# An event-driven list scheduler, DMA issues placed by their buffer, and weights copied back over three passes, in an eight-core encoder layer

## The chip, the cores and the metric

The kernel runs on all 8 NeuronCores of one Trainium2 chip, two of the 16 streams on each core, no exchange between cores. The metric is the device time of the slowest core in microseconds. Some executions here fell in a slower state, one die at a clearly lower granted TensorE clock (0.81 to 0.82 against 0.97 on the other die). In the lines of the profile PE is TensorE, PEld its loading of weights, DVE VectorE, ACT ScalarE and POOL GpSimd; SPq and POOLq are the queues of instructions in which SyncE (SP) and GpSimd issue DMA transfers. The granted clock is the clock that the profile records for TensorE, as a share of full speed.

## The reference, cut to what matters

```python
def layer(x, ...):                       # x: (B, T, 1024)
    z = rmsnorm(x, g_pre_mix) @ w_in     # 1024 -> 6 x 1024: xa, ga, u, v, two merge gates
    # branch A: width-4 causal conv -> RG-LRU scan over time -> * gelu(ga) -> @ w_br_a
    # branch B: gelu(u) * (Ws_masked @ LN(gelu(v)) + b_s), 128-position chunks -> @ w_br_b
    mix = (sigmoid(g_a) * o_a + sigmoid(g_b) * o_b) @ w_out
    x = x + rmsnorm(mix, g_post_mix)
    gate, up = split(rmsnorm(x, g_pre_ffn) @ w_ffn_in)          # 2 x 2816
    return x + rmsnorm((silu(gate) * up) @ w_ffn_out, g_post_ffn)
```

A core works on 4096 prompt rows and 64 sample rows, cut into nine tiles of 3 or 4 chunks of 128 rows. All weights, 70 pieces of at most 128 x 2048 elements, pass through a ring of 8 buffers once per tile. They lie in HBM in float32 (`wall`); a load from there casts to bf16 on the way (in the profile before 12.4 us, the median, from issue to landing). A bf16 copy (`wsc`) is written back to HBM in an early pass, and later tiles load that (4.6 us).

## The kernel before: the parts that the change touches

A recorder builds the program once without weights in time, to fix an order of stages, and replays that order. Each stage is a closure that appends instructions to in-order lists, one for each engine; semaphore waits follow from which buffers an instruction reads and writes.

```python
def load(i, pid):                                   # a piece into a ring buffer
    slot = free.popleft()
    if pid in cached:
        dma("sp", ...out=wring[slot], in_=wsc[pid]...)      # cached bf16 copy, by SP
        return
    dma("pool", ...out=wring[slot], in_=wall[pid]...)       # cast load, by GpSimd
    if seen[pid] == pid % 2:                                # copy back in pass 0 or 1
        cached.add(pid); todo_wo[i] = (slot, pid, n)

def fill():                                         # before every stage: as soon as a slot is released
    while not dry and free and W["next"] < len(stream):
        load(W["next"], stream[W["next"]]); W["next"] += 1

def acquire(pid):                                   # strictly in the order of the dry run
    assert stream[i] == pid
    if i in todo_wo: dma("sp", ...out=wsc[pid], in_=wring[slot]...)   # copy back at first use
...
def xr(s):       # x again, into the residual buffer x1 that the y store of the last tile reads
    dma("sp", ...out=x1[s], in_=x_rows(T, s)...)
put("xr", ("xr", t, s), xr, after=[("fb", t - 1, min(s, pns - 1))])
...
def gev(c):      # ScalarE: two gate tanh, then two exponentials, chunk by chunk
    tanh(E); tanh(I); exp(A, E); exp(E, E)
...
order = record(Prog(), None); P = Prog(); record(P, order)      # dry run, then replay
```

The constants of the spatial gate are loaded and multiplied out (16 pairs of small f32 matmuls, 64 records in the trace) before the first projection.

## Time and profile before

| | kernel before |
|---|---|
| median | 2448.1 us of 3 runs (2435.85 to 2545.6, the last a slow one) |
| TensorE busy, idle (core 0, 2440.1 us) | 2134 us, 306 us |
| mean granted clock, all cores | 0.951 to 0.957 |
| loads of weights | 105 cast, 525 cached, 70 copies back |

### The profile page before, as it was taken

What the parts mean: (1) busy time and instruction counts of PE and PEld (TensorE: products, weight loads), DVE (VectorE), ACT (ScalarE), POOL (GpSimd) and SP (SyncE); (2) the same over time, 40 slices, a digit from 0 to 9 for tenths busy, and PEclk for the clock granted to TensorE, in tenths of its full rate; (3) what the DMA queues carried; (4) which work ended last, traced back from release to release, by engine and by line L of the source; (5) the groups of instructions that cost most, each with busy time, mean ns of one, the idle gap of its engine ahead of it and who ended that gap; (6) DMA issues with size and microseconds to landing.
All of it is one profiled execution on the core that took longest, in us unless ns stands there. A gap on an engine that the chain in (4) does not pass through costs nothing.

```text
span 2440.1 us, 35711 instructions; the slowest of 8 cores (2422.7 to 2440.1 us)
## 1 busy us (share of the span) xinstructions
PE 2134.1 (87%) x10708; PEld 1037.8 (43%) x10708; DVE 1120.7 (46%) x1710; ACT 978.6 (40%) x1595; POOL 588.2 (24%) x966
## 2 busy tenths in 40 slices
PE   3788799679898899989998999899989988699795
PEld 2333344234343444434443444455545544354352
DVE  2653662116831386227832484258238427642231
ACT  2743651216612294126712481256229126611210
POOL 2213411234102240044104310331132033203302
PEclk9989899889998999999999999999999999899898
DMA  8588599885696544463545554556665664356351
GB/s 185 116 154 177 129 198 198 175 236 136 164 220 185 190 153 142 153 209 113 165 158 176 175 173 151 184 186 217 200 207 191 200 231 137 101 178 215 121 177 52
DMA packets 117308, 416.68 MB, mean 171 GB/s; under 512 B 14465, under 2 KB 14465, under 8 KB 117122
## 3 DMA queue, kind: packets, MB, share of 16 engines
q1 hardware_dynamic: 96592, 341.73, 43.2%
q0 software_dynamic: 19808, 71.05, 16.4%
q8 instruction: 92, 1.51, 0.3%
q10 hardware_dynamic: 722, 1.62, 0.2%
q14 instruction: 94, 0.77, 0.1%
HBM read 414.79 MB, written 53.54 MB: 192 GB/s over the span
## 4 chain that ended last, share of the span: by engine, by line
PE 67%; DMA 11%; DVE 6%; POOL 5%; ACT 5%; issue 5%; SPq 0%; DVEq 0%; POOLq 0%; ACTq 0%
PE ps L647 45%; PE ps L1126 11%; DMA wring<-wall 4%; PE ps L1031 4%; PE ps L868 4%; DMA wsc<-wring 2%; DMA wring<-wsc 2%; DVE xcf L750 1%; PE ps L602 1%; POOL x L1162 1%; DVE chI L803 1%; POOL stats L585 1%; DMA yp<-x 1%; DMA gvf<-rows 1%; POOL x L1157 1%
## 5 line engine op out<-in xcount | busy, mean ns | idle before, releaser
L647 PE MATMUL ps<-xnT,wring 128*128 128x512 bf16 (+2 forms) x2880 | 652.2, 377 | 109.5 <-DMA wring<-wsc 38.0
L647 PE MATMUL ps<-hnT,wring 128*128 128x512 bf16 (+2 forms) x3168 | 630.5, 361 | 13.4 <-DVE hnT L607 7.2
L647 PEld LDWEIGHTS ps<-xnT,wring 128*128 128x128 bf16 x2880 | 287.0, 101 | 418.5 <-issue 175.7
L647 PEld LDWEIGHTS ps<-hnT,wring 128*128 128x128 bf16 x3168 | 310.5, 98 | 323.7 <-issue 23.5
L1126 PE MATMUL ps<-wring,ffT 128*128 128x512 bf16 (+1 forms) x1452 | 318.7, 379 | 5.3 <-DMA wring<-wall 5.3
L1105 ACT ACTIVATE sgt<-ps 128x512 f32<-128x512 f32 (+2 forms) x198 | 109.0, 555 | 404.6 <-PE ps L647 392.8
L996 DVE SCALAR_TENSOR_TENSOR ffT<-ffT,ps 128x512 f32<-128x512 f32 (+2 forms) x144 | 88.8, 633 | 318.9 <-PE ps L647 246.0
L1109 DVE SCALAR_TENSOR_TENSOR sgt<-sgt,ps 128x512 f32<-128x512 f32 (+2 forms) x198 | 125.4, 633 | 222.8 <-PE ps L647 220.9
L987 ACT ACTIVATE ffT<-ps 128x512 f32<-128x512 f32 (+2 forms) x144 | 78.7, 553 | 357.6 <-PE ps L647 301.3
L1126 PEld LDWEIGHTS ps<-wring,ffT 128*128 128x128 bf16 (+1 forms) x1452 | 140.0, 98 | 182.1 <-issue 18.9
L750 DVE SCALAR_TENSOR_TENSOR xcf<-xa,vecs_sb,xcf 128x512 f32<-128x512 f32 (+2 forms) x240 | 161.0, 671 | 25.7 <-DVE xcf L750 0.5
L578 POOL TENSOR_SCALAR stats<-stats 128x1 f32<-128x1 f32 (+1 forms) x132 | 40.6, 308 | 526.5 <-ACT ffT L591 476.3
L1111 DVE SCALAR_TENSOR_TENSOR ffT<-sgt,ps 128x512 bf16<-128x512 f32 (+2 forms) x198 | 125.9, 636 | 41.1 <-PE ps L647 37.5
L1002 POOL TENSOR_TENSOR vnm<-ffT 128x512 bf16<-128x512 f32 (+2 forms) x72 | 83.8, 1164 | 248.3 <-DVE ffT L996 160.0
L647 PE MATMUL ps<-gsT,wring 128*128 128x512 bf16 (+2 forms) x576 | 131.7, 374 | 13.1 <-DVE gsT L950 5.2
L462 POOL DMA_DIRECT2D wring<-wall x105 | 58.9, 565 | 318.1 <-PE ps L647 274.1
L647 PE MATMUL ps<-hgT,wring 128*128 128x512 bf16 (+2 forms) x576 | 127.2, 365 | 4.1 <-DVE ffT L996 2.3
L1031 PE MATMUL ps<-wring,vnm 128*128 128x512 bf16 (+1 forms) x528 | 120.2, 384 | 3.2 <-POOL vnm L1002 2.5
L868 PE MATMUL ps<-wring,xnT 128*128 128x512 bf16 (+1 forms) x528 | 120.0, 382 | 1.4 <-ACT gga L823 1.4
L585 POOL TENSOR_TENSOR stats<-stats,nhalf 128x1 f32<-128x1 f32 x165 | 106.7, 647 | 25.4 <-POOL stats L578 1.0
L1153 DVE SCALAR_TENSOR_TENSOR tok<-ps,stats,gbc_pf 128x512 f32<-128x512 f32 (+1 forms) x33 | 24.6, 747 | 169.7 <-POOL stats L585 103.3
L1134 DVE COPY gvf<-ps 128x512 f32<-128x512 f32 (+1 forms) x33 | 22.0, 688 | 157.3 <-PE ps L1126 144.1
(113 smaller groups left out, 2230.0 us busy)
## 6 DMA issues: line engine op xcount, KB each, us to landing
wring<-wsc SPq DMA_DIRECT2D x511, 512.0 KB, 4.6
wring<-wall POOLq DMA_DIRECT2D x101, 512.0 KB, 12.4
wsc<-wring SPq DMA_DIRECT2D x68, 512.0 KB, 9.4
x<-xp SPq DMA_DIRECT2D x32, 512.0 KB, 4.6
yp<-x POOLq DMA_DIRECT2D x32, 512.0 KB, 3.7
xin<-xp SPq DMA_DIRECT2D x28, 512.0 KB, 5.8
wring<-wsc SPq DMA_DIRECT2D x14, 256.0 KB, 3.2
wring<-wall POOLq DMA_DIRECT2D x4, 256.0 KB, 14.2
```

The costliest lines, as they stand in the source:

```text
L585: pool(lambda e: e.tensor_tensor(out=stats[0:PT, r2:r2 + 1], in0=stats[0:PT, r:r + 1], in1=nhalf[0:PT, :], op=ALU.pow), 180, [("st", r), ( ...
L647: mm(lambda e, k=k: e.matmul(ps[:, b, 0:nt], lhsT=wv[:, k, m * 128:(m + 1) * 128], rhs=rhsT[:, k, 0:nt], start=(k == 0), stop=(k == NCH - ...
L750: dve(lambda e, k=k, dst=dst, win=win: e.scalar_tensor_tensor(out=dst, in0=win(k), scalar=vecs[:, V_CW + k, c:c + 1], in1=dst, op0=ALU.mul ...
L868: mm(lambda e, k=k, wv=wv, b=b: e.matmul(ps[0:PT, b, :], lhsT=xnT[:, k, col:col + PT], rhs=wv[:, k % 4, :], start=(k == 0), stop=(k == NCH ...
L987: act(lambda e: e.activation(out=tsig[i][:, 0:nt], in_=ps[:, b, 0:nt], func=AF.Tanh, scale=0.5), nt, [("ps", b)], c_tsig(i))
L996: dve(lambda e: e.scalar_tensor_tensor(out=mtmp[m][:, 0:nt], in0=tsig[i][:, 0:nt], scalar=1.0, in1=ps[:, b, 0:nt], op0=ALU.add, op1=ALU.mu ...
L1002: pool(lambda e: e.tensor_tensor(out=mixT[:, c, 0:nt], in0=mtmp[a][:, 0:nt], in1=mtmp[b][:, 0:nt], op=ALU.add), nt, c_mtmp(a) + c_mtmp(b), ...
L1031: mm(lambda e, k=k, n=n, wv=wv: e.matmul(ps[0:PT, pr + n, :], lhsT=mixT[:, k, col:col + PT], rhs=wv[:, k % 4, :], start=(k == 0), stop=(k ...
L1105: act(lambda e: e.activation(out=sgt[:, i, 0:nt], in_=ps[:, b, 0:nt], func=AF.Tanh, scale=0.5), nt, [("ps", b)], [("sgt", i)])
L1109: dve(lambda e: e.scalar_tensor_tensor(out=sgt[:, i, 0:nt], in0=sgt[:, i, 0:nt], scalar=1.0, in1=ps[:, bg, 0:nt], op0=ALU.add, op1=ALU.mul ...
L1111: dve(lambda e: e.scalar_tensor_tensor(out=ffT[:, j, 0:nt], in0=sgt[:, i, 0:nt], scalar=0.5, in1=ps[:, bu, 0:nt], op0=ALU.mult, op1=ALU.mu ...
L1126: mm(lambda e, j=j, kk=kk, b=b, PT=PT, col=col: e.matmul(ps[0:PT, b, :], lhsT=ffT[:, j, col:col + PT], rhs=wv[:, kk, :], start=(j == 0), s ...
```

## The change

Its intent: every engine takes, at each step, the stage that can start first (ties by a priority list); a DMA is put into its queue only when the model says its buffer is free; weight pieces may be used in any order in which they have landed; copies back are spread over three passes; x comes before the constants.

```diff
+def PASS_OF(pid):
+    return pid % 3
...
             def fill():
...
-                while not dry and free and W["next"] < len(stream):
+                at = P.free["pe"]
+                most = 0 if ("xsq", 0, 1) not in done else 2 if ("xsq", 0, 3) not in done else len(stream)
+                while wo and P.ready([("wr", wo[0])]) <= at:
+                    copy_back(wo.popleft())
+                while free and W["next"] < most and P.idle_from(("wr", free[0])) <= at:
...
             def acquire(pid):
-                assert stream[i] == pid
+                slot = have[pid].popleft()          # whichever piece has been loaded
+                if slot in todo_wo:
+                    wo.append(slot)                 # copy back later, when landed, at the latest when released
...
...
-                    put("xr", ("xr", t, s), lambda s=s: xr(s), after=[...])
+                    put("xr", ("xr", t, s), lambda s=s: xr(s), idle=lambda s=s: ("x1", s), after=[...])
...
+                def gex(c):                         # the two exponentials, now a stage of their own
...
-            order = record(Prog(), None)            # replay a fixed order
+            while True:                             # in the dry run and in the real one
+                fill()
+                for e in P.ENGS:
+                    on = [(r, PRI.index(n), q) ...  # stages open on this engine, earliest start r
+                    start = max(P.free[e], min(z[0] for z in on))
+                    best = ... min((z for z in on if z[0] <= start), key=priority + switch)
+                emit(best)
```

`switch` adds 8 places to the rank of a stage that would need another ScalarE table. For the first tile the scaling of x moves to VectorE, the carry copy of the scan moves from GpSimd to VectorE, and the spatial constants are built with 11 small f32 matmuls, after the first projections.

## The prediction

> **What bounds the kernel now.** I read the span of every core first (2422.7 to 2440.1 us, granted clock 0.951 to 0.957, both dies alike, so the profile is an undisturbed execution), then the busy shares, then stretches of the span, then the gaps of TensorE one by one, then what the DMA-issuing queue SP waits for.
>
> ```profile
> span 2440.1 us, 35711 instructions; the slowest of 8 cores (2422.7 to 2440.1 us)
> PE 2134.1 (87%) x10708; PEld 1037.8 (43%) x10708; DVE 1120.7 (46%) x1710; ACT 978.6 (40%) x1595; POOL 588.2 (24%) x966
> q1 hardware_dynamic: 96592, 341.73, 43.2%
> q0 software_dynamic: 19808, 71.05, 16.4%
> wring<-wall POOLq DMA_DIRECT2D x101, 512.0 KB, 12.4
> ```
>
> TensorE is idle for 2440 - 2134 = 306 us. A long run of 512-column matmuls goes at 215.8 ns each (288 in 62.16 us in the chain of waits) and of 384 columns at 162 ns (24 in 3.90 us). With the counts of the groups by shape: 6588 x 0.2158 = 1422; 2448 x 0.162 = 398; 816 of 448 columns x 0.189 = 154; 768 of 128 columns at about 0.056 = 43; 18 us of f32 setup. That is 2035 us, so of the 2134 busy us about 99 are matmuls at a slow clock. Idle plus slow clock, 405 us, is all that a reordering can win; the work itself does not shrink.
>
> The same counts split by stretches. I cut where the transposes of a tile's FFN input begin, since the work between two cuts is one tile's FFN and the next tile's branches.
>
> ```profile
> 0.00:61.00 61.00, 21.99 (x96) 17.70 (x96) 13.40 (x34) 15.36 (x22) 17.64 (x35) 1.00 0.86 185
> 61.00:76.00 15.00, 9.12 (x29) 3.47 (x29) 5.70 (x9) 5.97 (x10) 4.76 (x10) 0.90 0.66 202
> 76.00:122.00 46.00, 37.52 (x156) 15.75 (x154) 32.95 (x51) 39.41 (x57) 11.38 (x30) 0.91 0.50 88
> ...
> 367.00:460.00 93.00, 86.73 (x396) 37.79 (x395) 20.54 (x30) 12.59 (x25) 9.52 (x18) 1.00 0.99 197
> 460.00:548.00 88.00, 59.55 (x228) 23.84 (x227) 15.32 (x23) 17.60 (x31) 34.30 (x45) 0.79 0.81 210
> 548.00:837.00 289.00, 257.90 (x1217) 116.74 (x1215) 133.23 (x184) 111.94 (x178) 70.92 (x113) 0.95 0.66 182
> 837.00:1104.00 267.00, 253.77 (x1221) 116.10 (x1220) 132.20 (x184) 117.22 (x182) 63.85 (x98) 0.98 0.50 160
> ```
>
> Columns are busy us of PE, PEld, DVE, ACT and POOL, then granted clock, DMA share, GB/s. The reader is to see three regimes: a start in which PE does nothing useful for 61 us; a stretch to about 548 us in which DMA is at 0.5 to 1.0 and PE stops for it; and a steady state at a DMA share of 0.5 in which a tile still takes 267 us for about 247 us of matmuls (1120 of 512 columns x 0.2158 = 242, plus 5 of small ones).
>
> The gaps and their causes, from the timeline and the queue's waits:
>
> ```profile
> 43.06 0.76 PE L551 MATMUL ps<-gvf 128*128 128x128 f32 x2 [21.70 <-DMA gvf<-rows]
> ```
>
> ```profile
> 783.71 3.57 PE L647 MATMUL ps<-xnT,wring 128*128 128x512 bf16 x8 [10.18 <-ACT ffT L987]
> 788.16 15.23 SPq L695 DMA_DIRECT2D x<-xp  x4
> 803.54 37.98 SPq L459 DMA_DIRECT2D wring<-wsc  x16
> 809.83 3.30 PE L647 MATMUL ps<-xnT,wring 128*128 128x512 bf16 x8 [4.80 <-DMA wring<-wsc]
> ```
>
> ```profile
> SPq L199 <- DMA wring<-wall: 269.4, 32, 30.3
> SPq L199 <- DMA yp<-x: 121.5, 28, 6.2
> SPq L199 <- POOL x L1162: 70.1, 17, 15.6
> ```
>
> SP is one in-order queue. It holds weight loads, copies of cast weights back to HBM, and loads of x. At 788 us four loads of x wait in turn for the stores of y that free their buffer; the 16 weight loads behind them go out only at 803.5, and PE stops. Eight matmuls then take 3.30 us where they took 1.89. The 10.18 us gap before it is the same illness one step further: ScalarE sat 15 us in a square that waited for a late load of x, with the sigmoid that PE needed behind it. The 269 us are copies back that wait for their cast load to land, all before 548 us.
>
> [...] (0.79 granted in the stretch with most gaps; 3.57 against 1.89 us after the 10.18 us gap). So a removed gap is worth its length plus some 1.5 us. [...]
>
> **The change part by part.**
>
> 1. Cost of a piece of weights. Queue q1 took 43.2% of 2440 = 1054 us for 341.7 MB, 3.08 us per MB, so a 0.524 MB load from the cache is 1.6 us. q0 took 400 us; 17 MB of y at the same rate are 52; the rest over 105 cast loads is 3.3 us each.
>
> 2. Caching spread over three passes (index modulo 3) in place of two. Cast loads go from 105 to 24 + 2 x 23 + 3 x 23 = 139, cached loads from 525 to 491, copies back stay 70. That adds 34 x (3.3 - 1.6) = 58 us of engine time in all. But it is moved: up to the second cut (548 us) the kernel before has 88 cast loads (290), 18 cached loads and 53 copies (114), 16 transfers of x and y (26): 430, and the stretches sum to 448 with the constants. After: 94 cast (310), 12 + 36 (77), 26, together 413. In the next phase demand rises from about 194 to 234 us, then from 138 to 174.
>
> 3. The start. Gone are the wait of 21.70 us and the 64 f32 matmuls (18 us); x comes first, its scaling moves to VectorE, and weights begin right behind two tiles of x. Four loads of x are 6.6 us, the transposes end near 15 us, the first weight piece lands at 13 to 16. PE starts projections near 18 us instead of 61, but then eats a piece of two chunks in 3.5 us and the DMA brings one in 3.3. So the 43 us are not kept as PE time; they are kept as 43 us of earlier DMA.
>
> 4. Up to the second cut PE needs 2 x 123 + 114 + about 30 of transposes and cold clock = 390 us, DMA 413 + 8 of constants. DMA sets the end. I take a 0.90 share, between the 0.82 of before (448/548) and the 0.99 of its best stretch: 421/0.90 = 468. Won: 80 us.
>
> 5. Issues placed where the buffer is free: a load of x1 no longer stands in front of weights, copies back wait in a list until landed, POOL no longer holds 274 us of waits for PE in front of its arithmetic. From 548 us on the gaps that trace to this (10.2+0.8+4.8, 2.7+4.2, 6.7, 6.3, 9.0, 8.4, 5.2) sum to 58; seven groups x about 2 us of cold clock add 14. The third phase is up against 234 us of DMA in some 270, so I give it 17 and the others together 66: 83 of gaps, clock and small ACT waits.
>
> 6. Gated exponentials as their own stage with a penalty for table switches: 131 loads x 1.283 = 168 us on ACT, which is at 40%. Counted only inside part 5. The carry copy of the scan moves from POOL (365 ns x 72) to VectorE: 26 us off one queue, some 10 on another, off the path.
>
> 7. The last tile (150 us from its transposes) has nothing to overlap with and stays.
>
> Sum 80 + 83 = 163 if all goes well: 2277. A greedy order that takes whichever stage can start first will also make some bad choices which the old order did not; I keep three quarters, 122 to 130 us: **2312 us**.
>
> **The rivals.** (a) DMA stays the bound longer: at a share of 0.82 the second cut falls at 513 instead of 468 and phase three near 285; then about 2375. For it: 34 more cast loads, and their 12.4 us median to landing against 4.6. Against: 100 us of DMA idleness before 548 that SP's waits explain. (b) The new order is worse in the steady state: branches and FFN interleave less well, VectorE (132 of 267 us, but 51 of 61 in its densest stretch) or ACT (56 of 61) becomes the local bound, a tile stays at 267, and only the start is won: about 2360; if it loses 10 us per tile, 2430. For it: the model behind the list knows no cold clock. Against: the FFN is still there to fill. (c) Everything works, pieces in any order fill the DMA at 0.97 and tiles come to 252 us: 2250.
>
> **Range and chances.** 2250 to 2390 spans (c) to (a) plus a bad tile or two. Faster by over 2% needs under about 2395: 0.84. Within 2%: 0.12. Slower: 0.04.
>
> **What would show it.** Projections of the first tile beginning by 15 to 25 us; second cut near 470 with a DMA share of about 0.9; SP's waits for y stores and cast loads nearly gone; steady tiles at 253 to 259 with PE idle under 8 us each; mean clock 0.965 or more; PE idle 306 falling to about 200; 139 cast loads. Wrong if the second cut stays beyond 510 (part 4), if the 4 to 9 us gaps at the tile change return under another name (part 5), or if third-phase DMA waits exceed 20 us (part 2).

## More of the kernel before

The columns are waiting engine, tile and line, "<-" what it waited for, then the total in us, how often, and the longest one:

```profile
PE ps L602 <- ACT ffT L596: 41.8, 14, 10.0
PE ps L647 <- DMA wring<-wsc: 39.2, 10, 9.0
PE ps L647 <- ACT ffT L987: 31.2, 7, 10.2
PE ps L768 <- ACT xcb L761: 25.2, 11, 6.2
```

Waits for cached weights are only 39.2 of 306 us.

## The result, and the profile after

Ratios here are the mean time of one kernel's fast runs over that of the kernel before in the same rounds, so not quite the ratio of the medians (they are those of the record; recomputed from the fast runs listed there they come out the same within 0.001).

| | before | after |
|---|---|---|
| median of its runs | 2442.53 us (4 runs) | 2284.95 us (2280.78 to 2289.14, 4 runs) |
| ratio, 95% interval | | 0.9361 (0.930 to 0.9423): faster |
| the same kernel again on another chip (the control below) | 2433.62 us | 2266.7 us, ratio 0.9312 (0.9278 to 0.9346) |

On the first chip one die ran the changed kernel at a granted clock near 0.955 and the other at 0.973, in all its runs. In the control most of that difference is gone (profiled run 2239.8 to 2271.2 us, clock 0.960 to 0.975). Which cause this had on the first chip stays open. I read the changed kernel on core 0, which lies on the faster die there (2250.7 us, clock 0.972), beside core 0 of before (2440.1 us). Core 0 is the slowest core of before, so its gain of 189 us is above the average: the mean span of the eight cores is 2429.8 us before, 2258.8 after and 2255.9 in the control.

The best first view is the span cut where the tiles meet. A line that is easy to find in both traces is the first projection of a tile, which waits for its transposed input. In the prediction I called the cut "the transposes of a tile's FFN input"; looked at again they are the transposes of the next tile's input. The numbers stand, the name was wrong. The mark used from here on, the projection behind them, comes some 5.5 us later. Differences of the marks, core 0, in us:

| stretch | before | after | control |
|---|---|---|---|
| start to first tile change | 221.2 | 191.4 | 186.7 |
| second | 332.5 | 285.5 | 283.8 |
| third | 289.3 | 270.7 | 271.1 |
| fourth, fifth (4 chunks) | 266.5, 264.0 | 253.9, 251.4 | 252.8, 251.4 |
| sixth to eighth | 236.4, 205.2, 206.2 | 226.1, 192.3, 193.8 | 224.1, 192.5, 194.3 |
| the rest | 418.8 | 385.6 | 383.2 |

So of 189 us, 77 are won up to the second change (553.7 to 476.9), 19 in the third stretch, 61 in the five steady ones, 33 in the rest. As means over the eight cores, from before to the control, these are 72 (550.6 to 478.8), 11 (287.0 to 276.3), 60 and 31. Of core 0's 189 us, 133 are idle time of TensorE (306 to 173) and 56 are busy time (2134.1 to 2077.6): 13 of these are the smaller setup (22.2 to 9.2 us of f32 matmuls), the rest I put down to the granted clock, 0.972 after 0.951. Cutting the rest once more, where the last tile's FFN input is transposed, the last tile alone takes 151 us before (from 2289.5 us) and 154 after (from 2097.2); the 33 are all ahead of it. From the second change to that last cut, core 0 of before has 15 gaps of TensorE of 3 us or more; after has none.

The first projections, after, and the stretches that answer to those of before:

```profile
16.44 1.01 PE L661 MATMUL ps<-identb,ffT 128*128 128x128 bf16 x8 [0.34 <-DVE hcn L543]
21.95 2.29 PE L709 MATMUL ps<-xnT,wring 128*128 128x512 bf16 x5 [4.49 <-DVE xnT L666]
```

```profile
0.00:61.00 61.00, 31.44 (x136) 14.23 (x136) 35.82 (x55) 26.78 (x44) 19.05 (x49) 0.92 0.90 182
...
192.00:476.00 284.00, 256.16 (x1215) 116.63 (x1212) 135.55 (x191) 106.60 (x173) 91.13 (x146) 0.95 0.90 190
...
752.00:1005.00 253.00, 247.47 (x1214) 113.99 (x1213) 133.42 (x192) 109.48 (x175) 63.43 (x101) 1.00 0.67 193
1005.00:1256.00 251.00, 247.43 (x1212) 114.34 (x1211) 133.36 (x192) 108.18 (x174) 56.66 (x86) 1.00 0.53 168
```

Projections start at 22 us in place of 61. Up to 476.9 us the DMA is busy for 412 us (predicted 421), a share of 0.86 where the prediction assumed 0.90; from 192 us on it is 0.90. The steady tiles have 3.6 to 5.5 us of TensorE idle and the clock at 1.00: 251 us for a tile that needs about 247 of matmuls.

Now the queue. At the tile change that the prediction showed at 788 us, four loads of x stood in one block in front of all weights. After, first at the same change (695 us), then one change later, on core 0:

```profile
695.11 9.59 SPq L757 DMA_DIRECT2D x<-xp  x3
704.85 0.33 SPq L472 DMA_DIRECT2D wring<-wsc  x1
...
952.07 0.33 SPq L757 DMA_DIRECT2D x<-xp  x1
952.55 0.33 SPq L472 DMA_DIRECT2D wring<-wsc  x1
960.15 2.30 SPq L757 DMA_DIRECT2D x<-xp  x2
962.60 3.15 SPq L472 DMA_DIRECT2D wring<-wsc  x4
972.07 0.33 SPq L757 DMA_DIRECT2D x<-xp  x1
972.55 27.58 SPq L472 DMA_DIRECT2D wring<-wsc  x10
```

At 695 us three loads of x still wait in one block, but TensorE waits at most 1.54 us for a weight there (690 to 765 us). At 952 us the loads of x are spread between the weight loads. But the totals of what the queue waits for hardly moved:

```profile
SPq L208 <- DMA wring<-wall: 262.5, 27, 30.5
...
SPq L208 <- DMA yp<-x: 108.6, 27, 13.1
```

Those were 269.4 and 121.5 us before. I had predicted them "nearly gone". GpSimd's wait for TensorE in front of cast loads is also still there (first before, core 0, then after, core 5):

```profile
POOL wring L462 <- PE ps L647: 274.1, 57, 32.1
...
POOL wring L475 <- PE ps L709: 287.9, 67, 15.8
```

And on ScalarE the table loads fell from 131 to 82, 49 x 1.283 = 63 us of ACT time. Two groups of before, then the two that answer to them after, both on core 0; columns are line, count, busy us, mean ns, idle before:

```profile
L780 ACT ACT_TABLE_LOAD x47 | 60.3, 1283 | 0.8
L823 ACT ACT_TABLE_LOAD x43 | 55.2, 1283 | 3.8 <-PE ps L647 3.1
```

```profile
L848 ACT ACT_TABLE_LOAD x26 | 33.4, 1283 | 0.5
...
L889 ACT ACT_TABLE_LOAD x9 | 11.5, 1283 | 2.2 <-DVE hgT L882 2.1
```

L780 and L848 are the exponentials, L823 and L889 the gelus of the gate and of u, before and after. The one switch that I followed cost the load, 1.28 us, and next to nothing beside it: after, on core 0, one activation ends at 1011.50 us, the load runs from 1011.51, and the next begins at 1012.81.

So the result raised three questions. Which of the placements matters, if the waits stayed? What did ScalarE's new order bring? And is the DMA really the bound up to 476 us?

### The profile page after: what moved, and what is told of

The parts are those of the page before. It is cut to its first block, busy times and chain, and to the rows that moved or that the text cites. A ratio compares the mean times of both kernels' runs of the same rounds, so it can differ in the third digit from the quotient of the medians.

```text
span 2279.2 us, 34916 instructions; the slowest of 8 cores (2236.7 to 2279.2 us)
## 1 busy us (share of the span) xinstructions
PE 2119.9 (93%) x10666; PEld 1028.3 (45%) x10666; DVE 1141.7 (50%) x1782; ACT 916.6 (40%) x1542; POOL 576.0 (25%) x928
## 3 DMA queue, kind: packets, MB, share of 16 engines
HBM read 432.62 MB, written 53.54 MB: 213 GB/s over the span
## 4 chain that ended last, share of the span: by engine, by line
PE 80%; DMA 6%; POOL 4%; DVE 4%; issue 3%; ACT 3%; SPq 0%; DVEq 0%; POOLq 0%; ACTq 0%
PE ps L709 55%; PE ps L1194 14%; PE ps L936 4%; PE ps L1099 4%; DMA wring<-wall 2%; DMA wring<-wsc 2%; PE ps L661 1%; PE ps L830 1%; POOL x L1123 1%; DVE xnT L666 1%; DVE hnT L666 1%; POOL x L1230 1%; PE ps L997 1%; DMA wsc<-wring 1%; DVE xcf L812 1%
## 5 line engine op out<-in xcount | busy, mean ns | idle before, releaser
L709 PE MATMUL ps<-xnT,wring 128*128 128x512 bf16 (+2 forms) x2880 | 644.6, 372 | 44.3 <-DVE xnT L666 17.6
L709 PE MATMUL ps<-hnT,wring 128*128 128x512 bf16 (+2 forms) x3168 | 649.0, 366 | 12.4 <-DMA wring<-wall 5.8
L475 POOL DMA_DIRECT2D wring<-wall x139 | 78.0, 563 | 420.3 <-PE ps L709 287.9
L869 DVE TENSOR_TENSOR_SCAN chI<-chA,hst,chI 128x512 f32<-128x512 f32 (+1 forms) x72 | 87.0, 1208 | 7.5
```

Source lines behind the costliest of these rows:

```text
L709: mm(lambda e, k=k: e.matmul(ps[:, b, 0:nt], lhsT=wv[:, k, m * 128:(m + 1) * 128], rhs=rhsT[:, k, 0:nt], start=(k == 0), stop=(k == NCH - ...
L869: dve(lambda e: e.tensor_tensor_scan(out=chI[:, j, 0:np_], data0=chA[:, j, 0:np_], data1=chI[:, j, 0:np_], initial=hst[:, c:c + 1], op0=AL ...
```

## The experiments

The runs were on three chips; each shares its rounds with the kernel before on its own chip (medians 2439.27, 2433.62 and 2434.15 us), so ratios to before are what is compared across them. The control's 0.9312 is the yardstick. A hundredth of the ratio is 24 us. Two variants on the other two chips come within 0.002 of it (0.9306 and 0.9292), which speaks for comparing ratios across chips. Where means over eight cores are given, they are from each run's profiled execution, with the marks of the table above.

**Control: the changed kernel, unaltered.**

> The changed kernel itself, unaltered, as the control on this chip: its first runs had one die at a slightly lower granted clock (0.955 against 0.973), which none of the four experiments on another chip showed. Theory (that was the chip, not the change): 2250 to 2265 us with both dies at 0.97, ratio to before 0.924 to 0.930. Rival (the changed kernel draws the clock down on one die): 2285 us again.

2266.7 us, ratio 0.9312, four fast runs of 2258.73 to 2272.8. Between the two outcomes written down, nearer the first: the large difference between dies belonged to the first chip's runs.

**Loads of x offered at once (undone in the changed kernel).**

```diff
-put("xl", ..., idle=lambda s=s: ("xin", rot.get("xin", 0) % 2), after=...)
-put("xr", ..., idle=lambda s=s: ("x1", s), after=...)
+put("xl", ..., after=...)
+put("xr", ..., after=...)
```

> Changed kernel with one thing undone: the loads of x (into the input buffer and into the residual buffer) are offered as soon as their stage opens, not only once the buffer is free in the model. TensorE and VectorE keep exactly the order of the changed kernel; only the order inside the DMA queue and a few neighbours move. Theory A (the gaps at each tile change came from loads of x standing in front of weight loads): the gaps of 4 to 9 us behind weight loads return at six or seven tile changes, +25 to +60 us (2310 to 2345 us). Rival B (the steady gain comes from the new order of work on the engines, and the place of the x loads is worth little): under +10 us.

Ratio 0.940 (0.9372 to 0.9427), so 0.0088 or some 21 us above the control (11 to 32 by the two intervals): between the two. TensorE and VectorE have the same order of instructions as in the changed kernel. The trace shows where; core 1 of the ungated kernel, then of the control:

```profile
PE ps L709 <- DMA wring<-wsc: 45.4, 12, 9.4
...
PE ps L709 <- DMA wring<-wsc: 8.4, 7, 3.7
```

As means over the eight cores the third stretch grew by 5 us against the control, the fourth by 3, the sixth by 5, the seventh and the eighth by 4 each; the fifth and the rest did not. The new order already puts single weight loads between the loads of x; I take this to be why the gate is worth a third of the 57 us that the next run shows for the fault in the old order.

**Loads of x moved behind the weights (done alone in the kernel before).**

```diff
-put("xr", ("xr", t, s), xr, after=[("fb", t - 1, min(s, pns - 1))])
+put("xr", ("xr", t, s), xr, after=[("fb", t - 1, min(s, pns - 1)), ("ma", t, 7)])
```

> Kernel before with one thing moved: the loads of x into the residual buffer enter the DMA queue only after the last merge-gate projection of the tile, so behind the weight loads they used to block. All compute engines keep the exact order of the kernel before; only the DMA queue differs. Theory A: the gaps behind cached weight loads at tile changes (4.8, 4.2, 6.7, 9.0, 5.2 us, and the stretch behind each at slow clock) go, -30 to -50 us (ratio to before 0.980 to 0.988). Rival B (order of work is what won): -10 us or less, because another wait takes the same place.

2380.21 us, ratio 0.9768 (0.9743 to 0.9793): 57 us, more than expected, with every compute engine in the order of the kernel before. Only the DMA queue's order differs. At the same tile change the 15 weight loads now go first and the four loads of x need 1.89 us, not 15.23:

```profile
758.75 57.53 SPq L459 DMA_DIRECT2D wring<-wsc  x15
816.43 1.89 SPq L695 DMA_DIRECT2D x<-xp  x4
```

and TensorE's wait for cached weights is 0.7 us in one wait on core 5, where it was 29.1 in seven (on core 0, 0.5 in one for 39.2 in ten):

```profile
PE ps L647 <- DMA wring<-wsc: 0.7, 1, 0.7
```

On core 0 these 39 us of waits were worth 65 us (2440.1 to 2375.2): idle time of TensorE fell by 40 us, and its busy time, for the same 10708 matmuls, by 25 (2134.1 to 2109.6), as the granted clock rose from 0.951 to 0.964. So slower matmuls cost another 25 us beside the 39 of waits, some 60%; behind the 4.80 us gap that the prediction shows, eight of them took 3.30 us in place of 1.89. The four-chunk tiles reach 259.9 and 255.2 us.

The prediction called the 10.18 us gap at 783 us "the same illness". It is not: TensorE's waits for that sigmoid stay. Core 0 of this run:

```profile
PE ps L647 <- ACT ffT L987: 34.3, 8, 12.1
764.48 1.06 ACT L591 ACTIVATE ffT<-xin 128x1024 bf16<-128x1024 f32 x1 [16.96 <-DMA xin<-xp]
```

They were 31.2 us in 7 waits. In the longest of them the square in front of the sigmoid waits for x in the input buffer `xin`, a load that this run doesn't move. The changed kernel has 1.5 us of such waits left, and none of the five single parts undone in it brings them back (0.3 to 4.3 us). Which part removed them stays open.

**Copies back at first use (undone in the changed kernel).**

```diff
-while wo and P.ready([("wr", wo[0])]) <= at:
+while wo:
...
-    wo.append(slot)
+    copy_back(slot)
```

> Changed kernel with copies back issued the moment a piece is taken for use, as in the kernel before, in place of waiting in a list until the cast has landed in the model. Theory A (copies back waiting for their cast load hold up loads of x and cached weights behind them): +8 to +25 us, nearly all before 752 us. Rival (the queue's 250 us of waits for cast loads stayed in the changed kernel and cost nothing there, since nothing behind them was urgent): within 6 us of the control.

Ratio 0.926 (0.9227 to 0.9292): not slower, 0.6% faster than the control on the same chip. That is little, but all eight cores have the second change earlier, at 455 to 468 us (mean 462.5) where the control has 468 to 496 (mean 478.8), and nothing after it differs by more than 2 us. Theory A falls here: the wait list costs some 15 us ahead of the second change.

**Copies back late (done alone in the kernel before).**

```diff
 def acquire(pid): ...
-    dma("sp", ...out=wsc[p_], in_=wring[s_]...)
+    late_wo[s_] = (p_, n)
 def release(slot):
+    if slot in late_wo: dma("sp", ...out=wsc[p_], in_=wring[slot]...)
```

> Kernel before with one thing moved: a copy back is issued when its piece is released, so long after the cast load landed, in place of at its first use. Theory A: the wait of 269 us for cast loads in the DMA queue nearly goes, loads of x come in time in the first two tiles, -15 to -40 us, all before 843 us. Rival: the copy now stands between a freed buffer and its next load (9 us each in the trace), so buffers turn over more slowly in the stretch where the DMA is the bound: 0 to +40 us.

Ratio 1.0013 (0.9993 to 1.0032): nothing. And the premise was wrong as well: up to 548 us the queue still waits 240.8 us for cast loads. I take it that in that stretch the queue runs ahead of everything, so wherever the copy stands, the queue reaches it before the load has landed. Since the waits stayed, the run shows that the place of the copies doesn't matter here, and not what the waits cost. But over all versions they go with no loss of time: 224 to 300 us in the other versions of the changed kernel (cores 0 and 2), and 310 to 329 in the two fastest, the last two below.

**Weight loads and listed copies queued as soon as a buffer is released (undone in the changed kernel).**

```diff
-while wo and P.ready([("wr", wo[0])]) <= at:
+while wo:
-while free and W["next"] < most and P.idle_from(("wr", free[0])) <= at:
+while free and W["next"] < most:
```

> Changed kernel with weight loads (and the copies back from their list) put into the queues as soon as a buffer is released, as in the kernel before, not once the buffer is free in the model. Theory A as first stated (the place of every issue counts, GpSimd's arithmetic stands behind cast loads that wait for TensorE): +10 to +30 us, mostly before 752 us. Rival (a weight load that waits in its queue holds up nothing urgent; only loads of x do): within 6 us of the control.

Ratio 0.9292 (0.9242 to 0.9341): the control's, within the interval. The rival holds. Of "DMA issues placed where their buffer is already free", the part for loads of x is worth something and the part for weights nothing that these runs can tell from zero.

**ScalarE's grouping undone.**

```diff
-SWITCH = 8
+SWITCH = 0
-put("gev", ..., lambda c=c: gev(c), ...)
-put("gex", ..., lambda c=c: gex(c), ...)
+put("gev", ..., lambda c=c: (gev(c), gex(c)), ... + ([("su_decay",)] if t == 0 else []))
+put("gex", ..., lambda c=c: None, ...)
```

> Changed kernel with ScalarE's grouping undone: the exponentials go out at once behind the gate activations of their chunk as in the kernel before, and no penalty for switching tables. Theory C (what the x loads do not explain of the steady gain, some 50 us of 95, most of it in the next-to-last stretch, comes from ScalarE: 82 table loads in place of 131 and activations in an order by need): table loads rise back above 110, +15 to +45 us, most of it in the tiles with three chunks and in the stretch with the sample rows. Rival D (the order by event on TensorE is what counts and finds its way around any ScalarE order): under +10 us although the loads rise.

2316.06 us, ratio 0.9509 (0.9467 to 0.955): 0.0197 or 48 us above the control, the largest effect of any single part that was undone. The size is theory C's, the place is not: table loads rose to 100, not above 110. The mean span of the eight cores is 53 us above the control's; 19 of them lie ahead of the second change (497.6 for 478.8), 6 in the third stretch, 21 in the five steady ones, 8 in the rest. The new waits are TensorE's for the normalised v and for the x transposes, both fed by ScalarE:

```profile
PE ps L997 <- DVE vnm L972: 29.7, 3, 19.6
PE ps L661 <- ACT ffT L655: 29.0, 8, 7.4
```

(core 4; on core 5 of the control they are 7.0 and 16.7 us). Most of the first is two waits in the first tile (on core 0, 19.66 and 5.84 us at 121 and 127 us). This run changed two things at once, the split of the exponentials and the penalty, and in the first tile it also put the decay constants ahead of the gate activations; which of them counts is open.

**Weight pieces taken strictly in the planned order.**

```diff
 if st.acq:
     n = len(st.acq)
+    if not dry and stream[W["acq"]:W["acq"] + n] != list(st.acq):
+        return None
```

> Changed kernel with one part undone: stages that take weights must take them in the exact order of the dry plan, as in the kernel before, in place of any piece that has landed. Theory (small freedom, since the plan and the replay agree from the third tile on): 0 to +15 us, all before the second cut at 476 us. Rival (taking pieces in any order is the main gain of the DMA-bound stretch): +25 us or more up to the second cut.

Two of its four runs fell in the slow state (2523.1 and 2572.9 us). The two fast ones are 2297.36 and 2295.7 us; five fast runs of before in the same rounds have a mean of 2431.9, and with its slowest one of 2450.76 included 2435.0. That makes 0.943 to 0.944, some 29 us above the control, with half the usual number of runs. Over the eight cores, ten of them lie in the fourth stretch (262.9 us, 252.9 in the control) and ten in the rest (394.4 against 384.9). Up to the second change little can be told: 482 to 490 us, where the control has 468 to 496. Neither expectation holds: it is more than my theory allowed, and not where either has it. The wait that grew is again for the normalised v (35.0 us in 7 waits on core 5, 7.0 in 3 in the control).

**Constants before the first projection.** This kernel gives a wrong y (relative error 0.26): moved this early, the load of the spatial matrix is overwritten by the building of the transposition identity, which borrows the same buffer (in the trace it begins at 15.21 us, after waiting 11.93 us for that load, and the copy out of the buffer follows at 17.23). Times stand, results don't.

```diff
-put("su_in", ("su_spat_in",), su_spat_in, after=[("xa", 0, 5), ("xsc", 0, 3)])
+put("su_in", ("su_spat_in",), su_spat_in, after=[("xl", 0, 3)])
 put("xa", ..., after=xn_ok + started + ([("su_add",)] if t == 0 else []) + ...)
```

> Changed kernel, but the spatial constants are loaded and worked out before the first projection, which waits for them, as in the kernel before; weights still begin right behind x. Theory (up to the second cut the DMA is the bound, so an early start is worth something only as earlier DMA, and the ring of 8 pieces fills during the wait): the first projection starts 20 to 35 us later, of which only 5 to 20 us remain at the second cut (476 us). Rival (the start is a straight chain on TensorE): 20 to 35 us remain to the end.

Ratio 0.9306 (0.9264 to 0.9347): the control's. The first projection comes at 33.0 us, 11 later, less than I meant to set; the second change is at 473 to 480 us on the eight cores (mean 476.5), in the control at 468 to 496 (478.8). None of the 11 us is left that could be told from this spread. A later start of TensorE is made good before the second change, as the theory has it; with 11 us the test was mild.

**All copies back in the first pass.**

```diff
-    return pid % 3
+    return 0
```

> Changed kernel, but every piece is copied back in the first pass over the weights: 70 cast loads in place of 139, 560 cached loads, 70 copies back all in the first tile. By the engine time per piece of the prediction (3.3 us cast, 1.6 us cached or copied) the DMA needs about 14 us more until the second tile's input is transposed (427 against 413) and about 96 us less in the next stretch. Theory (DMA sets the end up to about 476 us, TensorE later): first 476 us become 476 to 495, the third stretch (276 us) falls to 258 to 265, in all -15 to +5 us. Rival (copies back hold buffers and the queue, and that is why three passes were chosen): the first stretch grows by over 25 us and the whole is slower by 15 us or more.

2252.17 us, ratio 0.9241 (0.9214 to 0.9268), 0.8% under the control of another chip. The second change comes 10 us later (mean of the eight cores 488.7 us, control 478.8; the estimate was 14 us more of DMA), and the third stretch takes 252.6 us on every core (control 271 to 280): the demand moved out of it left it at the steady tile's length, better than the 258 I allowed. The estimate of engine time per piece carries this. It also means that three passes are not shown to be a gain: one pass is a little faster.

**Copies back by use of the piece.**

```diff
-    return pid % 3
+    return 0 if pid < 36 else 1 + pid % 2
```

> Changed kernel with another choice of when a piece is copied back: the 36 pieces of projections, branches and output in pass 0 (they are wanted again within the same DMA-bound stretch), the 34 FFN pieces in pass 1 or 2 (not needed again before the second cut). Engine time by the prediction's 3.3 us cast and 1.6 us cached or copied: up to the second cut 36 x 6.5 + 34 x 3.3 + 26 = 372 us against 413; third stretch 223 against 234. Theory (the DMA sets the end up to the second cut at a share near 0.9): the cut moves from 476 to 430 to 450 us, total -25 to -45 us. Rival (what is left there is TensorE's own chain, the DMA only looks full because it prefetches): the cut stays within 10 us of 476 and the total too.

2232.53 us, ratio 0.9187 (0.9154 to 0.922), 1.3% under the control on the same chip. The second change comes at 449 to 463 us on the eight cores, mean 457.1 (control 468 to 496, mean 478.8), and the third stretch takes 259.5 us (276.3). Stretches of core 2, with the control's (also core 2) first and this kernel's second:

```profile
190.00:476.00 286.00, 257.15 (x1216) 117.01 (x1216) 135.65 (x192) 106.70 (x173) 90.74 (x146) 0.95 0.90 189
```

```profile
190.00:476.00 286.00, 276.38 (x1346) 127.69 (x1347) 151.14 (x215) 126.72 (x205) 95.44 (x149) 0.99 0.72 172
```

With less to fetch the DMA falls to 0.72 and TensorE rises to 276 of 286 us. (The second line reaches 27 us past this kernel's own second change at 449.4; up to there TensorE is busy for 249.78 of 259.40 us, and the DMA share is 0.76.) So the DMA was the bound in this stretch, and with this table of passes TensorE is. The cut stopped short of the 430 to 450 I expected; I put that down to TensorE's own 390 us and to the saturated first 190 us (DMA at 0.97).

**Both together, by use and at first use.**

> Both variants that were not slower than the changed kernel, together: copies back by use of the piece (0.9187 of before against the control's 0.9312) and copies back at first use (0.926). If the two act on the same stretch and the bound there is TensorE by now, the sum is no better than the first alone: 2225 to 2240 us. If they add: 2210 to 2222 us.

2225.37 us, ratio 0.913 (0.9084 to 0.9175), on yet another chip. The median sits at the edge of "no better than the first alone", the ratio 0.6% under it; its interval overlaps that of the table of passes alone. It is the fastest version that was run. The profiles show nothing that the second edit adds: the second change is at 455.9 us on the mean (457.1 with the table alone), the mean span 2214.3 us (2216.2).

## Why the prediction was right

2312 us with 2250 to 2390 was predicted, 2284.95 measured, 2266.7 in the control. The mechanism up to the second cut was right. Behind it, part of the gain is luck: some gaps went that the prediction put down to a wrong cause (4), and two parts that it gave no term of their own are worth 48 and 29 us (5). A deduction that the trace doesn't support (6) and a term that came out too small (5) left the number 27 to 45 us too slow, inside a wide range. By its own steps:

1. **Cost of a piece and the demand up to the second cut** (1, 2, 4): right. Predicted 421 us of DMA, a share of 0.90 and the cut at 468 us; the trace has 412 us, 0.864 over 476.9 us, and the cut, 5.5 us ahead of that mark, at 471. Both tables of passes that were tried moved the stretches the way the 3.3 and 1.6 us do. HBM reads show the larger transfer too: they rose from 414.79 to 432.62 MB with 34 loads cast in place of cached, 0.52 MB more for each.
2. **The start** (3): right. Projections predicted near 18 us and at most 25, measured 22; an 11 us later start left no trace at the second change.
3. **Third stretch**: 17 us predicted, 19 measured on core 0; the mean of the eight cores has 12, and 11 in the control. The sign of error set for it, over 20 us of DMA waits, did not come (9.2 us on core 0).
4. **Issues placed where the buffer is free** (5): the right phenomenon, a wrong reason for part of it. Loads of x in front of weights were the fault: moving them alone is worth 57 us in the kernel before, and a wait cost somewhat more slow clock beside its length than the 1.5 to 2 us that the prediction charged, an estimate from the 3.57 against 1.89 us behind one gap (25 us for ten). But of the waits from 548 us on 23 us, in six, were for the sigmoid behind the norm of the next x; they went for a reason that no run found. "Copies back wait in a list until landed" costs some 15 us, and "POOL no longer holds 274 us of waits" did not happen (287.9 us) and did not matter. "SP's waits for y stores and cast loads nearly gone" is the one stated sign that failed outright: 262.5 and 108.6 us remain. What changed is what stands behind the waits.
5. **Term that was mis-sized** (5 and 6): all stretches after the third, to which part 5 gave 66 us, won 94 on core 0 (84 on the mean of the eight cores, 91 in the control). The change to ScalarE's order was "counted only inside part 5"; undone alone it costs 48 us, a little over half of it in these stretches. Its 40% busy share had made it look harmless. Freedom in the order of pieces had no term of its own in the prediction and costs about 29 us when taken away.
6. **The haircut**: a quarter of the sum was taken off for bad choices of a greedy order. There were none to see in the steady tiles (251 us for 247 of matmuls). Without it the prediction was 2277, closer to the control's 2266.7.
7. **The last tile** (7): 151 and 154 us, unchanged as predicted.
8. **Rivals**: (a) needed a DMA share of 0.82, it was 0.86 to the cut and 0.90 in the second stretch; (b) needed tiles of 267 us, they take 251 to 254; (c) "tiles come to 252 us" is what happened to the tiles, and 2250.7 on the undisturbed die is its time.

Of the other signs, the 139 cast loads, the end of the gaps of 4 to 9 us at the tile changes and TensorE's idle time (173 us, about 200 predicted) came as written; the mean clock of 0.965 or more came on one die (0.971 to 0.976) and not on the other (0.952 to 0.958).

The single parts undone add up to 21 + 48 + 29 = 98 us of the 167 that the control gained over before. They may overlap, and they need not add. The rest was not taken apart: the step from two to three passes alone, the new start as a whole, and the order by event on TensorE itself. Of the 72 us up to the control's second change, undoing ScalarE's order brought back 19 and no other single undoing more than 7; whether the rest is the new start or the order by event is not shown.

## What to carry to other kernels

SyncE's DMA queue issued in order here (16 weight loads went out only after four loads of x had stood in front of them for 15.23 us): read each wait in such a queue by what stands behind it, not by its length. Waits of up to 15 us in front of weights cost 57 us in all, while the waits for cast loads in the same queue are longest (310 to 329 us) in the two fastest versions. When DMA bounds one stretch and not the next (a share of 0.90 and then 0.67 and 0.53 in the changed kernel), count engine time per transfer (here 3.3 us for a cast piece and 1.6 for a cached one, estimates from the busy shares of the two queues) and ask in which stretch each transfer is needed: another one-line table of who is cached when won another 1.3%. And ScalarE, busy for 40% of the span, was not harmless: undoing the order of its work cost 48 us.
